# First MLP layer of a transformer block on one core: token sums in two column steps, weight sums in place, a fourth and fifth bank for the first four pairs

## The chip, the cores and the metric

The kernel runs on one core of a Trainium2 chip, as one program. The metric is the device time of a launch in microseconds; the profile is one execution of the same program, recorded by the hardware. Engines are named as in the profile: PE multiplies matrices (PEld loads its weights), DVE, ACT and POOL work elementwise, SP issues the DMAs. Each engine takes its instructions in the order of its queue.

## The reference

One block of a streaming encoder on 1024 tokens of width 1024, in float32. Two attention branches are merged and projected; then comes the MLP, whose first layer the change touches:

```python
x = x + rms_norm(merged @ w_o[l], g_post_mix[l])
h = rms_norm(x, g_pre_mlp[l])
u = jnp.square(jax.nn.relu(h @ w_up[l]))        # w_up: 1024 x 4096
x = x + rms_norm(u @ w_down[l], g_post_mlp[l])
```

## The kernel before

**Precision.** Each operand of a product is kept as a rounded part (`hi`, cast by ACT) and the rest (`lo`, subtracted by DVE), and each product is three matmuls: hi by hi, hi by lo, lo by hi. `split` (L606) does both casts; its two lines are L607 and L608.

**The first layer with seven products.** `h @ w_up` is done in blocks of two by two: the weights of one pair of 128-column groups are A11, A12 (in the raw tile f0), A21, A22 (in f1); the tokens are B11, B12, B21, B22, where the first index is the half of the width and the second the half of the tokens. Instead of eight block products there are seven, of sums of blocks: the token sums T1 to T4 (`T1 = B12 - B11`, `T2 = B22 - T1`, `T3 = B22 - B12`, `T4 = B21 - T2`) are made once, the weight sums for each pair on POOL. A product of blocks is 12 matmuls of 512 columns. The results are put together in a pair by adds on DVE (v, q, u12, u21, u22), then relu and square on ACT. There are 16 pairs (`up_pair`, L768). The products B11 and B21 need only the first half of the tokens, so for the first four pairs (AHEAD) they are done early: each gives p1 (copied out of its bank by ACT, L737) and u11. `accs` there is in the two banks of tag "acc", and the B21 product goes on in the bank that p1 was copied from.

**What stands around the change.** `finish_tile` (L647) does the output projection of one 128-token tile: 48 matmuls, squares on ACT (L108), a scale factor on POOL (L116, L117), scaling and residual on DVE (L668, L669), squares of the result on ACT, a second factor on POOL (L114, L117), the scaling of h on DVE (L674), eight transposes on PE (L679), a copy on ACT (L681) and a store of the transposed blocks to `h_dram` (L682). After the eighth tile, all four token blocks are loaded again from `h_dram` (L753), T1 and T2 made on DVE, T3 and T4 on POOL, for each half q of the rows, and then POOL makes the first pair's weight sums (L772 to L775).

**Order.** The lines are scheduled by the framework before the launch, by its own time model; what comes out is a fixed queue for each engine with waits on semaphores. Tiles come from pools with a number of buffers (`bufs`); a tile whose buffer is still in use waits. The raw weight tiles have two buffers ("raw"), "row" four, "page" 24.

## Time and profile before

| | |
|---|---|
| median of 3 runs | 1512.61 us (1511.29 to 1513.62) |
| profiled execution | 1511.9 us, span 1510.2 us |
| mean granted TensorE clock | 0.983 |
| PE busy | 1442.4 us (96%) |
| DVE, ACT, POOL busy | 950.0, 740.0, 421.2 us |

All times below are of the profiled execution, from the start of its span. A wait names the instruction that came last by the profile. "x8" is a count of instructions in one row; the rows of a timeline that follow each other closely are merged. The clock is given as a share of 2.4 GHz, so 0.50 is 1.2 GHz.

### The profile page before, as it was taken

Reading aid. Unit: us, or ns where it says so; the run is one execution under the profiler, and the core shown is the slowest. Engines: PE = TensorE matmul, PEld = TensorE weight load, DVE = VectorE, ACT = ScalarE, POOL = GpSimd, SP = SyncE. Lnnn points to the kernel's source line nnn. Section 1 sums busy time; section 2 is a strip of 40 time slices with the busy share of each in tenths; the row PEclk is TensorE's granted clock in tenths of the full one; section 3 lists DMA queues with packets and bytes.
Section 4 is the critical chain, followed back from the end, with each engine's and each line's share of the span. In section 5 each row is a group of like instructions: output and inputs, shape, how many; then the busy total and the mean of one; then the engine's idle time right before and its main releaser. Section 6 shows DMA issues by size and latency. Waiting matters only on the chain. (4 is left out here: it accounts for less than half of the span.)

```text
span 1510.2 us, 20192 instructions
## 1 busy us (share of the span) xinstructions
PE 1442.4 (96%) x7314; PEld 1224.7 (81%) x7314; DVE 950.0 (63%) x1384; ACT 740.0 (49%) x1326; POOL 421.2 (28%) x382
## 2 busy tenths in 40 slices
PE   7999999999999999999999749999999999999993
PEld 6888998898889888888888538788888888888882
DVE  5478988898687857445544464444444587556526
ACT  6456766665565545843334433454445345344311
POOL 2022322220000000000011256766654563434205
PEclk9999999999999999999999869999999999999997
DMA  5332223121332253644367534444446775677615
GB/s 199 88 117 65 69 54 87 56 67 57 105 84 64 77 195 112 216 140 167 112 197 222 187 104 155 153 163 158 160 156 212 251 249 169 206 243 245 201 41 195
DMA packets 94411, 218.93 MB, mean 145 GB/s; under 512 B 9340, under 2 KB 25960, under 8 KB 94312
## 3 DMA queue, kind: packets, MB, share of 16 engines
q1 hardware_dynamic: 94312, 217.66, 44.9%
q8 instruction: 57, 0.93, 0.3%
q14 instruction: 42, 0.34, 0.1%
HBM read 151.28 MB, written 60.31 MB: 140 GB/s over the span
## 5 line engine op out<-in xcount | busy, mean ns | idle before, releaser
L198 PE MATMUL acc_gate<-h_hi,lo_gate 128*128 128x512 f32 x256 | 101.0, 394 | 0.0
L196 PE MATMUL acc_gate<-h_hi,hi_gate 128*128 128x512 f32 x256 | 100.9, 394 | 0.0
L197 PE MATMUL acc_gate<-h_lo,hi_gate 128*128 128x512 f32 x256 | 100.8, 394 | 0.0
L331 DVE TENSOR_TENSOR_SCAN rest<-rest 128x896 f32<-128x896 f32 (+3 forms) x64 | 87.6, 1373 | 20.6 <-POOL rest L326 20.3
L608 DVE TENSOR_TENSOR w_lo<-ws,w_hi 128x1024 fp32r<-128x1024 f32 x32 | 44.9, 1405 | 73.6 <-ACT w_hi L607 64.2
L326 POOL TENSOR_SCALAR_AFFINE_SELECT rest<-rest 128x128 f32<-128x128 f32 x64 | 23.5, 368 | 240.7 <-ACT rest L322 236.3
L608 DVE TENSOR_TENSOR lS_lo<-raw_S,lS_hi 128x1024 fp32r<-128x1024 f32 (+1 forms) x32 | 51.7, 1616 | 38.3 <-ACT lS_hi L607 38.3
L116 POOL TENSOR_SCALAR rstd_o<-s 128x1 f32<-128x1 f32 x8 | 2.8, 354 | 249.1 <-DMA xr<-in_x_dram 211.7
L607 ACT CAST lS_hi<-raw_S 128x1024 fp32r<-128x1024 f32 (+1 forms) x32 | 32.0, 1001 | 79.4 <-DMA raw_S<-s_dramS 43.6
L898 PE MATMUL dS<-rT_hi,lS_lo 128*128 128x512 f32 x180 | 70.0, 389 | 0.0
L898 PE MATMUL dS<-rT_lo,lS_hi 128*128 128x512 f32 x180 | 70.0, 389 | 0.0
L898 PE MATMUL dS<-rT_hi,lS_hi 128*128 128x512 f32 x180 | 70.0, 389 | 0.0
L567 PE MATMUL mix<-y,hi_mix 128*128 128x512 f32 x256 | 68.6, 389 | 0.0
L607 ACT CAST w_hi<-ws 128x1024 fp32r<-128x1024 f32 x32 | 33.5, 1046 | 69.8 <-POOL ws L773 60.9
L394 ACT ACTIVATE s<-s,low 128x896 f32<-128x896 f32 (+7 forms) x64 | 49.7, 777 | 29.7 <-DVE low L389 29.5
L375 POOL MEMSET bias<- 64x64 f32 x4 | 0.6, 144 | 214.4 <-DMA bias<-bias_rows 214.4
L389 DVE CUSTOM_DVE_ANT_0 s<-z,bias 128x512 f32<-128x512 f32 (+3 forms) x64 | 37.0, 586 | 32.4 <-PE z L263 26.6
L723 ACT ACTIVATE u<-u 128x512 f32<-128x512 f32 x48 | 30.2, 630 | 54.8 <-DVE u L802 33.7
L567 PEld LDWEIGHTS mix<-y,hi_mix 128*128 128x128 f32 x256 | 48.0, 188 | 10.0
L198 PEld LDWEIGHTS acc_gate<-h_hi,lo_gate 128*128 128x128 f32 x256 | 48.2, 188 | 9.2
L197 PEld LDWEIGHTS acc_gate<-h_lo,hi_gate 128*128 128x128 f32 x256 | 48.2, 188 | 8.8
L608 DVE TENSOR_TENSOR lA_lo<-raw_A,lA_hi 128x1024 fp32r<-128x1024 f32 (+1 forms) x24 | 35.5, 1478 | 31.4 <-ACT lA_hi L607 30.9
(341 smaller groups left out, 4896.9 us busy)
## 6 DMA issues: line engine op xcount, KB each, us to landing
raw_up<-in_w_up_dram SPq DMA_DIRECT2D x32, 512.0 KB, 3.9
s_dramS<-us SPq DMA_DIRECT2D x60, 256.0 KB, 2.0
raw_S<-s_dramS SPq DMA_DIRECT2D x28, 512.0 KB, 4.5
s_dramA<-u SPq DMA_DIRECT2D x49, 256.0 KB, 3.1
raw_A<-s_dramA SPq DMA_DIRECT2D x21, 512.0 KB, 3.7
raw_gate<-in_w_in_dram SPq DMA_DIRECT2D x16, 512.0 KB, 3.7
gate_dram<-gt SPq DMA_DIRECT2D x32, 256.0 KB, 2.5
y<-y_dram SPq DMA_DIRECT2D x16, 512.0 KB, 6.1
```

The costliest lines, as they stand in the source:

```text
L196: nc.tensor.matmul(acc, w_hi[:, ks], h_hi[k][:, cs], start=(k == 0), stop=False)
L197: nc.tensor.matmul(acc, w_hi[:, ks], h_lo[k][:, cs], start=False, stop=False)
L198: nc.tensor.matmul(acc, w_lo[:, ks], h_hi[k][:, cs], start=False, stop=(k == NK - 1))
L326: nc.gpsimd.affine_select(tl[:, dg], tl[:, dg], pattern=[[-1, P]], compare_op=ALU.is_gt, fill=fill, base=0, channel_multiplier=1,)
L331: nc.vector.tensor_tensor_scan(back, back, back, 1.0, op0=ALU.mult, op1=ALU.bypass)
L389: nc.vector.tensor_tensor_reduce(out=s[:, c0:c1], in0=z, in1=bias[:, S - nk + c0:S - nk + c1], scale=1.0, scalar=BIG if prev is None else ...
L394: e = nc.scalar.activation(s[:, :nk], s[:, :nk], AF.Exp, bias=low, scale=-1.0, accum_out=sums[:, m:m + 1],)
L567: nc.tensor.matmul(accs[i][c], st[:, ks], mv[:, cs], start=(first and k % 4 == 0), stop=(last and k % 4 == 3),)
L607: nc.scalar.copy(hi, raw)
L608: nc.vector.tensor_tensor(lo, raw, f32(hi), op=ALU.subtract)
L723: nc.scalar.activation(dst, src, AF.Relu)
L898: nc.tensor.matmul(accs[t], st[:, e, ts], mv[:, e, :], start=(pp == 0 and e == 0 and i == 0), stop=(pp == PP - 1 and i == 2),)
```

## The change

Five things change in the first layer.

- The token blocks are loaded while the last tile (t = 7) is still being worked on, in `load_h`: of the second token half only the columns of tiles 4 to 6 (EARLY, 384 columns). The last tile's transposes are copied by ACT from PSUM into the remaining 128 columns (LATE) of those tiles and aren't stored.
- All token sums are on DVE, first for the EARLY, then for the LATE columns. B22 and T2 come first, then T1, T3, T4. B11 and B21 blocks are loaded whole.
- The weight sums (`sums`) are made in place in the raw tiles f0 and f1, with one extra half tile s1; `split_sums` splits them. S1 is `w1`; f0 becomes S2 and S4 (`w24`), f1 becomes S3 and A22 (`w32`).
- The first pair's sums are made after tile 5's code, ahead of the early products.
- In the first four pairs, B22 and T4 have banks of their own (e and f, tag "acc") instead of going on in the banks of T1 and T3, the order of the products is T2, T1, B22, T3, T4, and the adds are regrouped. The later pairs keep their order.

The diff, without the branch of the later pairs, whose lines are as before but for the names of the weights:

```diff
@@ -657,6 +657,8 @@
                         accs[n], st, mv[:, n * HALF:(n + 1) * HALF],
                         start=(first and k == 0), stop=(last and k == NK - 1),
                     )
+        if t == NT - 1:
+            load_h()
         xt, o = row(f"xr_{t}"), row(f"or_{t}")
         nc.sync.dma_start(out=xt, in_=x[t * P:(t + 1) * P, :])
         s2 = pb.tile([P, 2], F32, tag="ssq", name=f"s2_{t}", bufs=4)
@@ -677,6 +679,10 @@
             for i in range(4):
                 k = 4 * j + i
                 nc.tensor.transpose(tr[:, i * P:(i + 1) * P], o[:, k * P:(k + 1) * P], ident)
+            if t == NT - 1:
+                for q in range(2):
+                    nc.scalar.copy(hraw[j, 1, q][:, :, LATE], tr[:, q * 256:(q + 1) * 256].rearrange("p (k t) -> p k t", k=2))
+                continue
             ht = tmp_tile(f"ht_{t}_{j}")
             nc.scalar.copy(ht, tr)
             nc.sync.dma_start(out=h_dram[j][c][:, :, ts], in_=ht.rearrange("p (k t) -> p k t", k=4))
@@ -693,6 +699,44 @@
         hi, lo = page(f"wa_hi{n}"), page(f"wa_lo{n}")
         split(hi, lo, raw)
         return hi, lo
+    EARLY, LATE = slice(0, HALF - P), slice(HALF - P, HALF)
+    hraw = {}
+    def load_h():
+        for q in range(2):
+            for j, c in ((0, 1), (0, 0), (1, 1), (1, 0)):
+                make = wide if q == 0 else pair_f32 if c else row_pair
+                hraw[j, c, q] = make(f"hraw{j}{c}{q}")
+                cs = EARLY if c else slice(0, HALF)
+                nc.sync.dma_start(out=hraw[j, c, q][:, :, cs], in_=h_block(j, c, q)[:, :, cs])
+    def pair_f32(name):
+        return pair_page(name, F32)
+    def row_pair(name):
+        return row(name, [P, 2, HALF])
+    def sums(n, s1):
+        f0, f1 = (raw_up(2 * n + i, f"up{n}_{i}") for i in range(2))
+        wa = None if n < AHEAD else split_f0(n, f0)
+        a11, a12, a21, a22 = (f[:, i * HALF:(i + 1) * HALF] for f in (f0, f1) for i in range(2))
+        nc.gpsimd.tensor_tensor(s1, a21, a22, op=ALU.add)
+        nc.gpsimd.tensor_tensor(a21, a11, a21, op=ALU.subtract)
+        nc.gpsimd.tensor_tensor(a11, s1, a11, op=ALU.subtract)
+        nc.gpsimd.tensor_tensor(a12, a12, a11, op=ALU.subtract)
+        return n, wa, s1, f0, f1
+    def split_sums(n, wa, s1, f0, f1):
+        w1 = pair_page(f"w1_{n}")
+        split(w1[:, 0, :], w1[:, 1, :], s1)
+        w24 = page(f"w24_hi{n}"), page(f"w24_lo{n}")
+        split(*w24, f0)
+        w32 = page(f"w32_hi{n}"), page(f"w32_lo{n}")
+        split(*w32, f1)
+        return wa, (w1[:, 0, :], w1[:, 1, :]), w24, w32
     first_a = []
     for t in range(NT):
@@ -706,6 +750,8 @@
                     split_h(name, q, raw)
             for n in range(AHEAD):
                 first_a.append(split_f0(n, raw_up(2 * n, f"ahead{n}")))
+        if t == 5:
+            sums0 = sums(0, stream.tile([P, HALF], F32, tag="tmp", name="s1_0", bufs=1))
     def product(acc, a, b, first=True):
@@ -740,76 +786,78 @@
             relu2(u11s[i][:, e, :], accs[e])
             state.append((p1s[i][:, e, :], u11s[i][:, e, :]))
-    def any_h_page(name):
-        made_h.append(name)
-        return big_pair(name) if len(made_h) <= 8 else pair_page(name)
-    made_h = []
-    for name in ("T2", "T1", "T3", "B22", "T4"):
-        h_pages(name, any_h_page)
-    for q in range(2):
-        b12, b11, b22, b21 = (wide(f"hraw_{n}{q}") for n in ("B12", "B11", "B22", "B21"))
-        for tile_, j, c in ((b12, 0, 1), (b11, 0, 0), (b22, 1, 1), (b21, 1, 0)):
-            nc.sync.dma_start(out=tile_, in_=h_block(j, c, q))
-        t2 = row(f"hraw_T2{q}", [P, 2, HALF])
-        nc.vector.tensor_tensor(b11, b12, b11, op=ALU.subtract)
-        nc.vector.tensor_tensor(t2, b22, b11, op=ALU.subtract)
-        split_h("T2", q, t2)
-        nc.gpsimd.tensor_tensor(b12, b22, b12, op=ALU.subtract)
-        split_h("T3", q, b12)
-        split_h("T1", q, b11)
-        split_h("B22", q, b22)
-        nc.gpsimd.tensor_tensor(b21, b21, t2, op=ALU.subtract)
-        split_h("T4", q, b21)
+    weights0 = split_sums(*sums0)
+    for name, make in (("B22", big_pair), ("T2", big_pair), ("T1", pair_page), ("T3", pair_page), ("T4", pair_page)):
+        h_pages(name, make)
+    for cs in (EARLY, LATE):
+        def split_part(name, q, raw):
+            hi, lo = hb[name][q]
+            split(hi[:, :, cs], lo[:, :, cs], raw)
+        hs = [[hraw[j, c, q][:, :, cs] for j, c in ((0, 1), (0, 0), (1, 1), (1, 0))] for q in range(2)]
+        for q, (b12, b11, b22, b21) in enumerate(hs):
+            nc.vector.tensor_tensor(b11, b12, b11, op=ALU.subtract)
+            split_part("B22", q, b22)
+            nc.vector.tensor_tensor(b12, b22, b12, op=ALU.subtract)
+            nc.vector.tensor_tensor(b22, b22, b11, op=ALU.subtract)
+            split_part("T2", q, b22)
+        for q, (b12, b11, b22, b21) in enumerate(hs):
+            split_part("T1", q, b11)
+        for q, (b12, b11, b22, b21) in enumerate(hs):
+            split_part("T3", q, b12)
+        for q, (b12, b11, b22, b21) in enumerate(hs):
+            nc.vector.tensor_tensor(b21, b21, b22, op=ALU.subtract)
+            split_part("T4", q, b21)
     STORED = ("A11", "S1", "S2", "A22", "S3", "S4", "A12")
     def up_pair(n):
-        f0, f1 = (raw_up(2 * n + i, f"up{n}_{i}") for i in range(2))
-        s12, s34 = (row(f"w{s}_{n}", [P, 2, HALF]) for s in ("s12", "s34"))
-        a11, a12, a21, a22 = (f[:, i * HALF:(i + 1) * HALF] for f in (f0, f1) for i in range(2))
-        nc.gpsimd.tensor_tensor(s12[:, 0, :], a21, a22, op=ALU.add)
-        nc.gpsimd.tensor_tensor(s12[:, 1, :], s12[:, 0, :], a11, op=ALU.subtract)
-        nc.gpsimd.tensor_tensor(s34[:, 0, :], a11, a21, op=ALU.subtract)
-        nc.gpsimd.tensor_tensor(s34[:, 1, :], a12, s12[:, 1, :], op=ALU.subtract)
         ahead = n < AHEAD
-        if not ahead:
-            wa = split_f0(n, f0)
-        w12 = page(f"w12_hi{n}"), page(f"w12_lo{n}")
-        split(*w12, s12.rearrange("p a b -> p (a b)"))
-        w34 = page(f"w34_hi{n}"), page(f"w34_lo{n}")
-        split(*w34, s34.rearrange("p a b -> p (a b)"))
-        w22 = pair_page(f"w22_{n}")
-        split(w22[:, 0, :], w22[:, 1, :], a22)
-        b, c, d = (bank(tag, f"p_{tag}{n}") for tag in BANKS[1:])
+        wa, w1, w24, w32 = weights0 if n == 0 else split_sums(*sums(n, row(f"s1_{n}", [P, HALF])))
         u1, u2 = wide(f"u1_{n}"), wide(f"u2_{n}")
         u12, u21, u22 = u1[:, 1, :], u2[:, 0, :], u2[:, 1, :]
+        v, q = tmp_tile(f"v_{n}"), tmp_tile(f"q_{n}")
+        b, c, d = (bank(tag, f"p_{tag}{n}") for tag in BANKS[1:])
         if ahead:
             p1, u11 = state[n]
+            e, f = (bank("acc", f"p{i}_{n}") for i in (3, 4))
+            product(b, blocks(w24, 0), "T2")
+            nc.vector.tensor_tensor(v, b, p1, op=ALU.add)
+            product(c, w1, "T1")
+            nc.vector.tensor_tensor(u12, c, v, op=ALU.add)
+            product(e, blocks(w24, 1), "B22")
+            nc.vector.tensor_tensor(u12, e, u12, op=ALU.add)
+            relu2(u12, u12)
+            product(d, blocks(w32, 0), "T3")
+            nc.vector.tensor_tensor(q, d, v, op=ALU.add)
+            nc.vector.tensor_tensor(u22, c, q, op=ALU.add)
+            relu2(u22, u22)
+            product(f, blocks(w32, 1), "T4")
+            nc.vector.tensor_tensor(u21, f, q, op=ALU.add)
+            relu2(u21, u21)
         else:
             u11 = u1[:, 0, :]
             a = bank("acc", f"c11_{n}")
             product(a, blocks(wa, 0), "B11")
             p1 = tmp1(f"p1_{n}")
             nc.scalar.copy(p1, a)
...
         parts = {"A11": u11, "A12": u21, "A22": u22}
         if n < UP - 1:
```


What the scheduler makes of it on POOL, around the last tile (`rstd_o7` and `rstd_x27` are its two scale factors, `raw_up0_1` the second raw weight tile of pair 0). First POOL's queue before:

```order
L117 TENSOR_TENSOR rstd_x26_8804<-rstd_x26_8804,neg_half_74 128x1
L116 TENSOR_SCALAR rstd_o7_8880<-s2_7_8877 128x1
L117 TENSOR_TENSOR rstd_o7_8880<-rstd_o7_8880,neg_half_74 128x1
L114 TENSOR_SCALAR rstd_x27_8889<-sx_7_8887 128x1
L117 TENSOR_TENSOR rstd_x27_8889<-rstd_x27_8889,neg_half_74 128x1
L758 TENSOR_TENSOR hraw_B120_9045<-hraw_B220_9047,hraw_B120_9045 128x1024
L762 TENSOR_TENSOR hraw_B210_9048<-hraw_B210_9048,hraw_T20_9053 128x1024
L758 TENSOR_TENSOR hraw_B121_9068<-hraw_B221_9070,hraw_B121_9068 128x1024
L772 TENSOR_TENSOR ws12_0_9095<-raw_up0_1_9093 128x512
```

Here the two factors follow each other, then come subtractions on token blocks and only then the sums of pair 0. POOL's queue at the same place after:

```order
L117 TENSOR_TENSOR rstd_x26_8813<-rstd_x26_8813,neg_half_74 128x1
L726 TENSOR_TENSOR s1_0_8739<-raw_up0_1_8742 128x512
L727 TENSOR_TENSOR raw_up0_1_8742<-raw_up0_0_8740,raw_up0_1_8742 128x512
L116 TENSOR_SCALAR rstd_o7_8905<-s2_7_8902 128x1
L728 TENSOR_TENSOR raw_up0_0_8740<-s1_0_8739,raw_up0_0_8740 128x512
L117 TENSOR_TENSOR rstd_o7_8905<-rstd_o7_8905,neg_half_74 128x1
L729 TENSOR_TENSOR raw_up0_0_8740<-raw_up0_0_8740 128x512
L114 TENSOR_SCALAR rstd_x27_8914<-sx_7_8912 128x1
L117 TENSOR_TENSOR rstd_x27_8914<-rstd_x27_8914,neg_half_74 128x1
L726 TENSOR_TENSOR s1_1_9229<-raw_up1_1_9232 128x512
```

Two of pair 0's four sums now stand ahead of the factor's first operation, one between its two operations and one behind; the subtractions on token blocks are gone from POOL.

On SP, the DMA queue, from the loads for the early products to the token blocks (`xr_7` is the last tile's x, `hraw` the token blocks, `x2_dram` where the residual is stored). First SP's queue before:

```order
L661 DMA xr_7_8874<-in_x_dram 128x1024
L689 DMA raw_ahead3_8563<-in_w_up_dram 128x1024
L682 DMA h_dram01_89<-ht_5_0_8728 512x1x128
L682 DMA h_dram11_91<-ht_5_1_8736 512x1x128
L670 DMA x2_dram_87<-xr_6_8789 128x1024
L689 DMA raw_up0_0_9091<-in_w_up_dram 128x1024
L689 DMA raw_up0_1_9093<-in_w_up_dram 128x1024
L682 DMA h_dram01_89<-ht_6_0_8813 512x1x128
L682 DMA h_dram11_91<-ht_6_1_8821 512x1x128
```

Here `xr_7` is loaded early and no token block yet. SP's queue at the same place after:

```order
L713 DMA hraw001_8893<-h_dram00_88 128x1024
L695 DMA raw_ahead3_8563<-in_w_up_dram 128x1024
L713 DMA hraw101_8897<-h_dram10_90 128x1024
L688 DMA h_dram01_89<-ht_5_0_8728 512x1x128
L688 DMA h_dram11_91<-ht_5_1_8736 512x1x128
L672 DMA x2_dram_87<-xr_6_8798 128x1024
L695 DMA raw_up0_0_8740<-in_w_up_dram 128x1024
L695 DMA raw_up0_1_8742<-in_w_up_dram 128x1024
L663 DMA xr_7_8899<-in_x_dram 128x1024
L688 DMA h_dram01_89<-ht_6_0_8822 512x1x128
L688 DMA h_dram11_91<-ht_6_1_8830 512x1x128
L713 DMA hraw010_8883<-h_dram01_89 128x2x384
```

Two whole token blocks now stand ahead of the raw weight loads of pair 0, and the load of `xr_7` has moved behind them.

On DVE, from the last tile's first scaling (L671 after, L669 before) on, with `hT20` and `hB220` the parts of T2 and B22 for q = 0. First DVE's queue before:

```order
L669 SCALAR_TENSOR_TENSOR xr_7_8874<-or_7_8875,rstd_o7_8880,xr_7_8874 128x1024
L674 SCALAR_TENSOR_TENSOR or_7_8875<-xr_7_8874,rstd_x27_8889,grow1_8179 128x1024
L755 TENSOR_TENSOR hraw_B110_9046<-hraw_B120_9045,hraw_B110_9046 128x1024
L756 TENSOR_TENSOR hraw_T20_9053<-hraw_B220_9047,hraw_B110_9046 128x1024
L608 TENSOR_TENSOR hT20_lo_9026<-hraw_T20_9053,hT20_hi_9025 128x1024
L608 TENSOR_TENSOR hT10_lo_9030<-hraw_B110_9046,hT10_hi_9029 128x1024
```

Here the scaling of h comes second, and the token sums only after it. DVE's queue at the same place after:

```order
L671 SCALAR_TENSOR_TENSOR xr_7_8899<-or_7_8900,rstd_o7_8905,xr_7_8899 128x1024
L800 TENSOR_TENSOR hraw000_8885<-hraw010_8883,hraw000_8885 128x2x384
L802 TENSOR_TENSOR hraw010_8883<-hraw110_8887,hraw010_8883 128x2x384
L676 SCALAR_TENSOR_TENSOR or_7_8900<-xr_7_8899,rstd_x27_8914,grow1_8179 128x1024
L608 TENSOR_TENSOR hB220_lo_9060<-hraw110_8887,hB220_hi_9059 128x2x384
L800 TENSOR_TENSOR hraw001_8893<-hraw011_8891,hraw001_8893 128x2x384
L803 TENSOR_TENSOR hraw110_8887<-hraw110_8887,hraw000_8885 128x2x384
L802 TENSOR_TENSOR hraw011_8891<-hraw111_8895,hraw011_8891 128x2x384
L810 TENSOR_TENSOR hraw100_8889<-hraw100_8889,hraw110_8887 128x2x384
L800 TENSOR_TENSOR hraw000_8885<-hraw010_8883,hraw000_8885 128x2x128
L800 TENSOR_TENSOR hraw001_8893<-hraw011_8891,hraw001_8893 128x2x128
```

Two EARLY subtractions stand ahead of the scaling of h (L676, before L674), and the sums of both steps are mixed with the splits.

## Rows read from the trace of the kernel before

**Rows 1.** The page's part 2: PE and its clock in 40 slices, tenths.
```profile
PE   7999999999999999999999749999999999999993
...
PEclk9999999999999999999999869999999999999997
```

**Rows 2.** Waits of PE, 858 to 1210 us: total, times, longest.
```profile
PE p_sc L717 <- ACT w_hi L607: 30.0, 1, 30.0
PE p_av L717 <- DVE u L802: 2.0, 2, 1.1
PE p_tr L717 <- DVE q L800: 0.4, 1, 0.4
PE p_sc L717 <- DVE w_lo L608: 0.3, 1, 0.3
```

**Rows 3.** Windows: busy (instructions) of PE, PEld, DVE, ACT, POOL; PE clock, DMA share, GB/s.
```profile
838.00:840.00 2.00, 2.00 (x10) 1.66 (x9) 0.94 (x1) 1.61 (x3) 0.00 (x0) 1.00 0.99 320
858.00:860.00 2.00, 0.06 (x1) 0.00 (x0) 0.89 (x2) 1.42 (x2) 2.00 (x1) 1.00 0.14 54
860.00:862.00 2.00, 0.00 (x0) 0.00 (x0) 2.00 (x2) 2.00 (x4) 2.00 (x2) 0.54 0.00 0
880.00:890.00 10.00, 1.90 (x4) 1.16 (x4) 9.94 (x5) 2.88 (x3) 9.10 (x4) 0.50 0.00 1
```

**Rows 4.** Chain that ended last, pieces from 835 to 895: start, us, what.
```profile
835.38 10.92 PE c L717 x48
...
866.30 5.90 DMA hraw_B<-h_dram
...
890.31 4.39 PE p_sc L717 x10
```

**Rows 5.** Timeline of DVE: start, us, line, operation, out<-in, idle before.
```profile
837.65 1.28 DVE L669 SCALAR_TENSOR_TENSOR xr<-or,rstd_o,xr 128x1024 f32<-128x1024 f32 x1 [0.34 <-POOL rstd_o L117]
841.11 1.28 DVE L674 SCALAR_TENSOR_TENSOR or<-xr,rstd_x,grow 128x1024 f32<-128x1024 f32 x1 [2.17 <-POOL rstd_x L117]
...
859.66 2.18 DVE L608 TENSOR_TENSOR hT_lo<-hraw_T,hT_hi 128x1024 fp32r<-128x1024 f32 x1 [1.11 <-ACT hT_hi L607]
...
867.33 1.21 DVE L608 TENSOR_TENSOR hT_lo<-hraw_B,hT_hi 128x1024 fp32r<-128x1024 f32 x1
...
891.43 0.68 DVE L608 TENSOR_TENSOR w<-raw_up,w 128x512 fp32r<-128x512 f32 x1
```

**Rows 6.** Timeline of ACT, last token tile.
```profile
838.97 1.06 ACT L108 ACTIVATE or<-xr 128x1024 f32<-128x1024 f32 x1 [0.23 <-DVE xr L669]
...
840.88 0.59 ACT L737 COPY p<-c 128x512 f32<-128x512 f32 x1 [0.76 <-PE c L717]
```

**Rows 7.** Timeline of POOL: a scale factor, then the first sum of five pairs.
```profile
836.68 0.30 POOL L116 TENSOR_SCALAR rstd_o<-s 128x1 f32<-128x1 f32 x1 [4.45 <-ACT or L108]
...
877.03 2.25 POOL L772 TENSOR_TENSOR ws<-raw_up 128x512 f32<-128x512 f32 x1
...
895.81 1.29 POOL L772 TENSOR_TENSOR ws<-raw_up 128x512 f32<-128x512 f32 x1 [6.63 <-DMA raw_up<-in_w_up_dram]
...
908.08 1.29 POOL L772 TENSOR_TENSOR ws<-raw_up 128x512 f32<-128x512 f32 x1 [7.14 <-DMA raw_up<-in_w_up_dram]
...
925.07 1.28 POOL L772 TENSOR_TENSOR ws<-raw_up 128x512 f32<-128x512 f32 x1 [4.96 <-DMA raw_up<-in_w_up_dram]
...
941.53 1.30 POOL L772 TENSOR_TENSOR ws<-raw_up 128x512 f32<-128x512 f32 x1 [4.39 <-DVE u L808]
```

**Rows 8.** SP issuing raw weight loads; single DMAs: KB, us to landing.
```profile
831.52 3.52 SPq L689 DMA_DIRECT2D raw_up<-in_w_up_dram  x2
...
raw_up<-in_w_up_dram SPq DMA_DIRECT2D x1, 512.0 KB, 4.8
...
h_dram<-ht SPq DMA_DIRECT2D x2, 256.0 KB, 5.2
...
hraw_B<-h_dram SPq DMA_DIRECT2D x2, 512.0 KB, 5.0
```

More of the change, by code (lines that the diff above doesn't have):

```diff
@@ L795, in up_pair @@
             nc.scalar.copy(p1, a)
-        product(b, blocks(w12, 1), "T2")
-        v, q = tmp_tile(f"v_{n}"), tmp_tile(f"q_{n}")
-        nc.vector.tensor_tensor(v, b, p1, op=ALU.add)
-        product(d, blocks(w34, 0), "T3")
-        nc.vector.tensor_tensor(q, d, v, op=ALU.add)
-        product(c, blocks(w12, 0), "T1")
-        nc.vector.tensor_tensor(u22, c, q, op=ALU.add)
-        relu2(u22, u22)
-        if not ahead:
+            product(b, blocks(w24, 0), "T2")
+            nc.vector.tensor_tensor(v, b, p1, op=ALU.add)
+            product(d, blocks(w32, 0), "T3")
+            nc.vector.tensor_tensor(q, d, v, op=ALU.add)
+            product(c, w1, "T1")
+            nc.vector.tensor_tensor(u22, c, q, op=ALU.add)
+            relu2(u22, u22)
             product(a, blocks(wa, 1), "B21", first=False)
             relu2(u11, a)
-        product(c, blocks(w34, 1), "B22", first=False)
-        nc.vector.tensor_tensor(u12, c, v, op=ALU.add)
-        relu2(u12, u12)
-        product(d, (w22[:, 0, :], w22[:, 1, :]), "T4", first=False)
-        nc.vector.tensor_tensor(u21, d, v, op=ALU.add)
-        relu2(u21, u21)
+            product(c, blocks(w24, 1), "B22", first=False)
+            nc.vector.tensor_tensor(u12, c, v, op=ALU.add)
+            relu2(u12, u12)
+            product(d, blocks(w32, 1), "T4", first=False)
+            nc.vector.tensor_tensor(u21, d, v, op=ALU.add)
+            relu2(u21, u21)
         parts = {"A11": u11, "A12": u21, "A22": u22}
```

## The prediction, made blind

> **What bounds the kernel now.** I read the page's forty slices first. PE is full nearly everywhere and dips once, in slices 23 and 24, where the granted clock dips with it [rows 1]. Then the waits of PE over the whole first MLP layer: of 32.7 us waited, 30.0 is one wait, for the cast of the first pair's weight sums, and 2.7 are three small ones in the next pairs [rows 2]. Then the windows and the chain through the gap: PE runs the 96 matmuls that need only the first token half, ending at 858.1; the second set of token blocks lands only at 866.30 + 5.90 = 872.2, POOL begins the first pair's weight sums at 877.03, and PE restarts at 890 - 1.9 = 888.1 [rows 3, 4, 7]. Last the clock: 1.00 in the 2 us in which PE's last matmul ended, 0.54 in the next two [rows 3]. After the gap the first 14 matmuls (4 before 890, then 10 in 4.39 us) take about 0.44 us each, against 10.92/48 = 0.2275 at full clock [rows 3, 4]: 14 x 0.21 = 3.0 us more. So this place costs 30.0 + 3.0 + 2.7 = 35.7 us, and outside it the layer is PE alone. That is all the change can win.
>
> **What goes.** The last token tile's transposes no longer travel out to memory and back; ACT copies them into the loaded blocks. Three quarters of the second half's columns (EARLY) and all of the first half are loaded before that tile is done, so the 5.0 and 5.9 us loads [rows 4, 8] leave the path. The eight subtractions of the token sums all go to DVE, so its splits no longer run beside POOL's: 2.18 us beside it, 1.21 alone [rows 5]. The first pair's weight sums move ahead of the gap. PE's work does not change: the number of products is the same, and the extra banks only reorder them.
>
> **What is put in the way: the last token tile.** Before, POOL did nothing around 836 but that tile's two scale factors: the first started at 836.68 and the DVE operation waiting for it at 837.65, 0.97 us later [rows 5, 7]. Now POOL's queue has two of the first pair's block sums ahead of that factor, one inside it and one behind it, and the first of them waits for the second raw weight load. That load is the last of two issued in a stretch that ends at 831.52 + 3.52 = 835.0, and took 4.8 us [rows 8]: 839.5. A 512 KB token block now goes ahead of it in SP's queue, while the DMA engines are 0.99 busy at 320 GB/s [rows 3]: 524/320 = 1.6 us, so 841. (Bounds: 839.5 if it fits into slack, 844 if two such transfers get ahead.) Three sums at 1.25 from start to start (895.81's 1.29 less overlap) and the 0.97: the DVE operation starts at 841 + 3.75 + 0.97 = 845.7, 8 us later than before. The tile's x rows, now loaded only behind that weight load (about 836), land by 842 at its 4.8 us and stay hidden; if they land after 845.7 the stall below grows by as much.
>
> What queues behind it is the cost. On ACT the tile's squares (1.06) stand ahead of the copy of the second early product (0.59), and PE may not overwrite that bank before the copy. Before, squares and copy were at 838.97 and 840.88, and PE never waited [rows 6]. Now the squares start 1.3 after DVE, at 847.0, and the copy ends at 848.6. PE reaches that place after 36 matmuls, 835.4 + 36 x 0.2275 = 843.6, so it waits **5.0 us** (bounds 2 and 9). Before, the clock fell about 2 us into an idle stretch and 14 matmuls then ran slow [rows 3, 4]; after 5 us I take the same **3.0 us** (bound below: 0).
>
> **The token sums themselves.** From the tile's last normalisation on DVE to the split that lets PE go beyond its first four new matmuls, DVE's queue has 10 operations of 768 columns, 12 of 256, one of 512 and one of 1024. By a line through 0.68 and 1.21 [rows 5] that is 10 x 0.95 + 12 x 0.42 + 0.68 + 1.21 = 16.6 us, less some 0.08 overlap each, about 15. Before, that normalisation started 2.14 us after the tile's squares (841.11 against 838.97 [rows 5, 6]), which would now be 849.1; and, new, two EARLY subtractions stand ahead of it and wait for the token loads. These follow the previous tile's stores (issued about 836.5, landing 5.2 later, 842) and land in pairs 5.0 later [rows 8]: 847 to 848. So it starts at about 849, ends at 850.3, and the split ends at 865.5 to 867. PE after its stall has 12 + 48 matmuls and 0.8 us of transposes: 848.6 + 60 x 0.2275 + 0.8 + 3.0 = 866.0. They meet: I take **0** for this wait, with 0 to 4 as bounds. If the front stall is absent PE comes at 858 and waits here instead, since DVE's 15 us do not shrink.
>
> **The first pairs.** The two raw buffers are now held until the split of the sums made in them. Before, the second buffer was already held until the last split, and it paced the pairs: POOL's first sum starts at 895.81, 908.08, 925.07 and 941.53, 12.3, 17.0 and 16.5 us apart, against 60 x 0.2275 = 13.7 of PE work per pair [rows 7]. PE's waits there were 2.7. That pacing stays as it was. New is that the second pair's sums come while DVE still splits T3 and T4, where a POOL operation takes 2.25 instead of 1.29 [rows 7]: four times 0.96 = 3.8 us later, some of it covered. With the slow-clock lead gone I take **3.6 us** of waits (bounds 1 and 10).
>
> One rule bears on this last point: the Trainium skill, "SBUF — State Buffer", section on who interferes with whom, says that a VectorE operation with two SBUF inputs and a GpSimd one that reads SBUF exclude each other, so one waits for the whole of the other. The trace agrees (2.18 and 2.25 where they meet). By the rule taken strictly, the six splits left by then (about 4.1 us) and the four sums (5.0) run one after the other, so the second pair's weights would come 4.1 us late, not 3.8, and the sum would change by 0.3.
>
> **Sum.** The new losses are 5.0 + 3.0 + 0 + 3.6 = 11.6 us against 35.7: 24.1 less. The profiled execution took 1511.9 (span 1510.2), so 1487.8; the median of the runs is 0.7 above the profiled one, so 1488 to 1488.5. The pairs from the fifth on have 84 matmuls, 19.1 us, and stay PE's.
>
> **Rivals.**
> 1. *The front is covered.* If the weight load lands at 839.5 and the sums run unhindered, DVE starts at 844.2, PE waits 3.5 us, and a shorter idle may leave the clock up, with 1 to 2 us of waiting at T2 instead: losses of 4 to 6, 1481 to 1483. For it: PE's waits of 1 us after the gap left the clock alone [rows 1, 2]. Against: the queue order is fixed, and DMA is full just there.
> 2. *The front is later, or the pairs are paced.* The load at 844 makes the stall 8; or pairs 1 to 3 run at the 16.7 of before instead of 13.7, 3 us each over three pairs: 9 instead of 3.6. Losses of 17 to 22: 1494 to 1499. For it: the measured 17.0 and 16.5. Against: with those PE waited only 2.7, because it does the next pairs' other products between.
> 3. *Slower: summing in place paces all later pairs.* One buffer's cycle is load, four sums, casts, splits, next load, with up to four POOL operations for the stored sums in between. Before, the last two of those four stood behind the cycle; put inside it they add 1.3 + 2.25 to 16.5, 20.0 against PE's 19.1, which over twelve pairs is 11 us (1499 in all). It makes the kernel slower only from 19.1 + 24/12 = 21.1 us per pair on, that is if most POOL operations also run at 2.25. Against: in the new order most later pairs have the four sums first, and a pair's weights are split almost a whole pair ahead.
> 4. *It doesn't do what it says*: T2 still needs the last tile, and if DVE's 15 us were not hidden behind the products, up to 16 of the 30 us would return: 1504. Only the queue's order, not the trace, says they are hidden.
>
> **How the numbers follow.** Forecast 0.62 (1485 to 1492 by its own bounds), rival 1 0.17, rival 2 0.13, rival 4 0.04, rival 3 0.04 (three quarters of it slower). The range 1480 to 1496 leaves out about 0.2. About 0.2% (3 us) is what can be told from no change: faster 0.95, same 0.02, slower 0.03.
>
> **What would show it.** In the new profile: PE's 30 us wait for a weight cast gone; one wait of about 5 us near 843 inside the early products, put down to ACT's copy, with the clock at half after it; POOL's first sum starting near 841, directly on the landing of a raw weight load; DVE's splits of the token sums near their uncontended length; T2 starting near 866 with little wait; 1 to 2 us waits in the second and third pairs; none from the fifth. The forecast is wrong if PE's losses between the last output-projection matmul and the fifth pair are under 7 or over 17 us, or if the later pairs take over 19.3 us each.

## The result, and the profile after

The changed kernel takes 1495.10 us (median of four runs, 1494.08 to 1498.55) against 1511.95 for the kernel before (1510.27 to 1513.62) beside it: a ratio of 0.9893, interval 0.9872 to 0.9913. It is 16.9 us faster; the forecast was 24. The time lies in the forecast's range of 1480 to 1496, at its upper end. The profiled execution took 1494.08 (span 1492.4).

The first page still shows where the place was: in place of the dip to 7 and 4 tenths [rows 1] there are two slices at 8 tenths with a full one between them, and the clock row no longer dips. The first of the two (821 to 858 us) holds the early products, the second (895 to 933 us) the third and fourth pair.

```profile
PE   7999999999999999999999898999999999999993
PEclk9999999999999999999999999999999999999997
```

The waits of PE from the last output projection through the first MLP layer, in the changed kernel (what it waited for: us in total, times, longest), against the 30.0 us of [rows 2]:

```profile
PE c L763 <- ACT p L783: 5.5, 1, 5.5
PE p_sc L763 <- ACT w_hi L607: 3.7, 2, 2.2
PE p_tr L763 <- DVE q L849: 1.2, 1, 1.2
PE p_av L763 <- ACT w L607: 1.1, 2, 0.7
PE p_sc L763 <- DVE w_lo L608: 1.0, 1, 1.0
PE p_av L763 <- DVE u L851: 0.7, 1, 0.7
PE trh L681 <- DVE or L676: 0.6, 1, 0.6
PE p_av L763 <- DVE w L608: 0.5, 1, 0.5
```

The first row belongs to the front (the last token tile among the early products). The seventh lies ahead of the early products, at the transposes of the tile before, where the kernel before waited 0.8 us. The other six, 8.2 us, lie in the pairs, where the forecast had 3.6: 6.3 of them come before the fifth pair, 1.9 behind its start.

The front, in the timeline of the changed kernel (start, us, engine, line, operation, in brackets the idle time before it and its releaser), one fence for each engine. POOL:

```profile
840.61 1.28 POOL L726 TENSOR_TENSOR s<-raw_up 128x512 f32<-128x512 f32 x1 [7.89 <-DMA xr<-in_x_dram]
843.36 0.30 POOL L116 TENSOR_SCALAR rstd_o<-s 128x1 f32<-128x1 f32 x1
...
845.49 1.26 POOL L729 TENSOR_TENSOR raw_up<-raw_up 128x512 f32<-128x512 f32 x1
```

DVE, ACT and PE behind it:

```profile
845.56 2.27 DVE L671 SCALAR_TENSOR_TENSOR xr<-or,rstd_o,xr 128x1024 f32<-128x1024 f32 x1 [7.75 <-POOL rstd_o L117]
847.87 1.06 ACT L108 ACTIVATE or<-xr 128x1024 f32<-128x1024 f32 x1 [8.62 <-DVE xr L671]
848.92 0.57 ACT L783 COPY p<-c 128x512 f32<-128x512 f32 x1
866.46 0.39 PE L763 MATMUL p_sc<-hT_hi,w_hi 128*128 128x512 f32 x1
```

POOL does two sums of the raw weights, then the scale factor with a third sum inside it. (The first row names the x rows, but the second raw weight tile, which this sum reads, was issued at 835.20 and landed 5.3 us later, at 840.5, just before the sum starts.) DVE waits for the factor, ACT's squares wait for DVE, and the copy of the product stands behind the squares. PE is back at 849.54 and reaches T2 at 866.46 without a wait. The clock in that stretch, by windows of the changed kernel (us, PE busy, PEld, DVE, ACT, POOL, PEclk, DMA share, GB/s):

```profile
845.00:850.00 5.00, 0.46 (x1) 0.46 (x2) 3.97 (x3) 2.13 (x4) 2.57 (x5) 0.76 1.02 353
850.00:855.00 5.00, 5.00 (x16) 3.84 (x16) 4.54 (x6) 1.48 (x4) 0.65 (x1) 0.55 0.79 279
919.40:922.50 3.10, 3.10 (x7) 2.48 (x8) 2.17 (x1) 0.00 (x0) 3.02 (x2) 0.50 0.85 242
```

After the 5.5 us wait 12 matmuls take 5.29 us in the chain, 2.6 more than at 0.2275 each. The third row is one pair's start, told below.

Losses are counted in one way from here on, from PE's timeline: the time that a stretch took, less its matmuls at 0.2267 us each (84 of them take 19.04 us in the later pairs, where PE waits for nothing). So a loss holds both PE's waits and what half clock costs. The front is the stretch from the start of the first early product to that of T2; its 96 matmuls and eight transposes (0.8 us) make 22.6 us. The pairs are counted from T2 on, the first four pairs (240 matmuls) by themselves. So counted, the front loses 8.1 us, the first four pairs 10.2 and the later ones 2.6, 20.9 together. Before, it was 30.3, 4.3 (most of it half clock behind the gap) and 3.5, or 38.1. The difference is 17.2; the measured gain is 16.9.

The pairs, POOL's first sum of each from the second on, in the changed kernel:

```profile
874.04 3.73 POOL L726 TENSOR_TENSOR s<-raw_up 128x512 f32<-128x512 f32 x1 [23.39 <-DVE hT_lo L608]
...
890.63 1.30 POOL L726 TENSOR_TENSOR s<-raw_up 128x512 f32<-128x512 f32 x1
891.89 1.31 POOL L867 TENSOR_TENSOR us<-us,u 128x512 f32<-128x512 f32 x1
...
894.85 1.30 POOL L869 TENSOR_TENSOR us<-u,us 128x512 f32<-128x512 f32 x1
...
909.83 1.29 POOL L726 TENSOR_TENSOR s<-raw_up 128x512 f32<-128x512 f32 x1 [3.98 <-DMA raw_up<-in_w_up_dram]
...
926.49 1.30 POOL L726 TENSOR_TENSOR s<-raw_up 128x512 f32<-128x512 f32 x1 [3.78 <-DMA raw_up<-in_w_up_dram]
```

The four sums (L726) stand 16.6, 19.2 and 16.7 us apart; in [rows 7] it was 12.3, 17.0 and 16.5. The fourth and the fifth wait for a transfer of raw weights. In the third pair two other sums, of the layer's results (L867, L869), stand between the pair's own, 2.6 us in all, as much as its 19.2 has over the others' 16.6. What lies between two of them, on ACT, DVE and SP's queue:

```profile
882.24 2.00 ACT L607 CAST w_hi<-raw_up 128x1024 fp32r<-128x1024 f32 x2 [3.81 <-POOL raw_up L729]
883.32 2.36 DVE L608 TENSOR_TENSOR w_lo<-raw_up,w_hi 128x1024 fp32r<-128x1024 f32 x2 [2.45 <-ACT w_hi L607]
884.57 1.46 SPq L695 DMA_DIRECT2D raw_up<-in_w_up_dram  x2
```

The sums end at 882.21; then two casts and two splits, and the third pair's loads go out from 884.57 on, as the splits end. Its sums start at 890.63. PE meets the end of that cycle three times (the same kernel's PE):

```profile
899.88 0.50 PE L763 MATMUL p_sc<-hT_hi,w_hi 128*128 128x512 f32 x1 [2.19 <-ACT w_hi L607]
917.18 0.50 PE L763 MATMUL p_sc<-hT_hi,w_hi 128*128 128x512 f32 x1 [1.53 <-ACT w_hi L607]
919.40 0.79 PE L763 MATMUL p_sc<-hT_hi,w_lo 128*128 128x512 f32 x1 [1.02 <-DVE w_lo L608]
```

The forecast's sum was 24.1 and about 17 came, so 7 us are missing. Two candidates: the front (8.1 against 8.0 forecast, a visible stall, behind which everything else stands), and the cycle of the two raw tiles, which summing in place holds until cast and split have read them.

### The profile page after: what moved, and what is told of

Same layout as the page of the kernel before. It is cut to its first block, busy times and chain, and to the rows that moved or that the text cites. A ratio compares the mean times of both kernels' runs of the same rounds, so it can differ in the third digit from the quotient of the medians.

```text
span 1492.4 us, 20173 instructions
## 1 busy us (share of the span) xinstructions
PE 1443.9 (97%) x7314; PEld 1224.5 (82%) x7314; DVE 955.7 (64%) x1410; ACT 739.4 (50%) x1338; POOL 414.4 (28%) x378
## 5 line engine op out<-in xcount | busy, mean ns | idle before, releaser
L608 DVE TENSOR_TENSOR w_lo<-raw_up,w_hi 128x1024 fp32r<-128x1024 f32 x32 | 44.4, 1397 | 49.8 <-ACT w_hi L607 43.3
L763 PE MATMUL c<-hB_hi,wa_hi 128*128 128x512 f32 x128 | 51.0, 398 | 5.5 <-ACT p L783 5.5
L196 PEld LDWEIGHTS acc_gate<-h_hi,hi_gate 128*128 128x128 f32 x256 | 48.2, 188 | 8.6
```

What stands on the lines that cost most here:

```text
L196: nc.tensor.matmul(acc, w_hi[:, ks], h_hi[k][:, cs], start=(k == 0), stop=False)
L608: nc.vector.tensor_tensor(lo, raw, f32(hi), op=ALU.subtract)
L763: nc.tensor.matmul(acc, st[:, ks], mv, start=(first and k == 0 and i == 0), stop=(k == 3 and i == 2), skip_group_check=True,)
```

## Experiments

Every ratio is against the kernel before, run beside it. Losses are in us, of the profiled execution, as counted above; the last column is the time in us from the start of the first early product (835.72 in the changed kernel) to that of T2 (866.46), so that it doesn't depend on when the stage began. The front's loss is this time less 22.6.

| run | us | ratio (95%) | front loss | first four pairs | later pairs | early products to T2 |
|---|---|---|---|---|---|---|
| changed kernel | 1495.10 | 0.9893 (0.9872 to 0.9913) | 8.1 | 10.2 | 2.6 | 30.7 |
| factors first | 1495.12 | 0.9891 (0.9875 to 0.9906) | 7.3 | 11.2 | 3.2 | 29.9 |
| two sets | 1484.35 | 0.9817 (0.9800 to 0.9833) | 8.3 | 3.9 | 0.1 | 30.9 |
| own tiles | 1487.70 | 0.9842 (0.9824 to 0.9860) | 8.5 | 6.1 | 0.4 | 31.1 |
| three banks | 1498.99 | 0.9915 (0.9900 to 0.9929) | 7.8 | 14.0 | 4.3 | 30.4 |
| last weights split in halves | 1494.55 | 0.9873 (0.9853 to 0.9893) | 7.9 | 6.7 | 5.8 | 30.5 |
| two tiles on chip | 1485.73 | 0.9818 (0.9797 to 0.9840) | 9.7 | 3.9 | 0.1 | 32.3 |
| blocks in pages | 1487.97 | 0.9832 (0.9815 to 0.9850) | 10.7 | 4.1 | 0.0 | 33.3 |
| tokens behind the tile | 1486.51 | 0.9821 (0.9804 to 0.9837) | 9.2 | 4.5 | 0.0 | 31.8 |
| sums before tokens | 1483.98 | 0.9817 (0.9801 to 0.9834) | 6.6 | 5.3 | 0.0 | 29.2 |

**The front alone: the scale factors ahead of the sums.** POOL does the last tile's two factors, then the first pair's four sums (`last_pow` is the operation that makes a factor, so in the end the last one).

```diff
-        if t == 5:
-            sums0 = sums(0, stream.tile([P, HALF], F32, tag="tmp", name="s1_0", bufs=1))
+    with tc.issue_after(getattr(last_pow[0], "ins", last_pow[0])):
+        sums0 = sums(0, stream.tile([P, HALF], F32, tag="tmp", name="s1_0", bufs=1))
...
```

> The first pair's four sums queue on POOL behind both factors of the last tile. Theory (the stall at the front only moves: T2 cannot start much before 865, because the token blocks land at 847 to 849 and DVE then has some 15 us of sums and splits, and the pairs behind it go at the pace of their raw buffers, 16.6 us): the 5.5 us wait for ACT's copy becomes about 3 us at the first copy, since the squares still wait for x (landing about 841), a new wait of 2 to 4 us stands ahead of T2, and the time falls by 0 to 2 us, to 1493 to 1495. Rival (the stall is a loss of its own): 5.5 us of wait and 2.4 us of half clock come back, 1487.

Measured: 1495.12, the time of the changed kernel. The wait that was to go got shorter and split up, as the waits of PE in this run show:

```profile
PE c L765 <- ACT p L785: 5.1, 2, 3.5
PE p_sc L765 <- ACT w_hi L609: 3.1, 2, 1.5
PE p_sc L765 <- DVE w_lo L610: 1.9, 2, 1.0
```

T2 comes 0.9 us sooner (29.86 against 30.73), and the pairs lose 1.6 more. So the sums inside the factor do cause part of the stall, but taking them out is worth nothing by itself, as the theory had it: PE comes sooner to work that isn't ready sooner.

**The pairs, a second set of raw tiles.** The second raw tile of every pair but the first gets its own memory (a free row tile), so that loads need no longer wait for the split of the pair before.

```diff
-        f0, f1 = (raw_up(2 * n + i, f"up{n}_{i}") for i in range(2))
+        f0 = raw_up(2 * n, f"up{n}_0")
+        if n == 0:
+            f1 = raw_up(1, "up0_1")
+        else:
+            f1 = row(f"raw_up{n}_1")
+            nc.sync.dma_start(out=f1, in_=w_up[2 * n + 1])
```

> From the second pair on, one of the two raw weight tiles is a row tile, so two pairs' weights are held at a time instead of one. Theory (pairs 1 to 3 are paced by load, four sums in place, casts, splits and the next load in one set of buffers, 16.6 to 19.2 us against 13.7 us of PE work): PE's waits from the second pair on fall from about 11 us with the half clock to 1 to 4, and the time to 1485 to 1488; the front stall of 5.5 us stays. Rival (POOL's eight sums a pair, or the contention with DVE, set the pace): the waits stay above 8 us, 1492 to 1495.

Measured: 1484.35, 10.7 us less than the changed kernel and just below what the theory gave, with the front as it was. The waits of PE:

```profile
PE c L768 <- ACT p L788: 5.3, 1, 5.3
PE c L768 <- DVE u L836: 1.3, 1, 1.3
PE p_tr L768 <- DVE hT_lo L608: 1.3, 1, 1.3
...
PE p_sc L768 <- DVE w_lo L608: 0.5, 1, 0.5
```

No wait of over 0.5 us for weights is left. The pairs' loss falls from 12.8 to 4.0, in the first four from 10.2 to 3.9. The rival (POOL's sums, or its contention with DVE, set the pace) is out: POOL does the same sums, and the first of them takes even longer here. POOL's sums of the second, third and fourth pair begin thus (the same run):

```profile
859.65 11.78 POOL L731 TENSOR_TENSOR s<-raw_up 128x512 f32<-128x512 f32 x1 [9.31 <-DMA raw_up<-in_w_up_dram]
880.75 1.29 POOL L731 TENSOR_TENSOR s<-raw_up 128x512 f32<-128x512 f32 x1 [3.97 <-DVE hT_lo L608]
887.14 1.30 POOL L731 TENSOR_TENSOR s<-raw_up 128x512 f32<-128x512 f32 x1 [1.17 <-DVE w_lo L608]
```

The third and fourth start 9.9 and 22.7 us earlier than at 890.63 and 909.83. The pacing by the raw tiles is gone.

**The pairs, sums in their own tiles again.** Pairs from the second on sum as before, into four own halves, and T2's weights are split from those; the rest of the change stays.

```diff
+        if n == 0:
...
+        s12, s34 = (row(f"w{s}_{n}", [P, 2, HALF]) for s in ("s12", "s34"))
+        nc.gpsimd.tensor_tensor(s12[:, 0, :], a21, a22, op=ALU.add)
+        nc.gpsimd.tensor_tensor(s12[:, 1, :], s12[:, 0, :], a11, op=ALU.subtract)
+        nc.gpsimd.tensor_tensor(s34[:, 0, :], a11, a21, op=ALU.subtract)
+        nc.gpsimd.tensor_tensor(s34[:, 1, :], a12, s12[:, 1, :], op=ALU.subtract)
+        return n, wa, s12, s34, a22
```

> From the second pair on the weight sums go into two tiles of their own, as in the kernel before, and the raw tiles are free as soon as they are read; all else stays changed. Theory (making the sums in place holds both raw tiles for a cast and a split longer, and T2 waits for all four sums): first sums of pairs 1 to 3 come 12 to 17 us apart again, PE's waits in these pairs fall by 4 to 7 us, 1488 to 1491. Rival (the first pairs wait only because PE now asks for them without a gap ahead; in place or not is the same): waits as in the changed kernel, 1493 to 1496.

Measured: 1487.70, 7.4 us less than the changed kernel, just below what the theory gave. The first sums of the pairs (POOL in this run) stand 16.4, 16.0 and 15.9 us apart:

```profile
877.45 3.59 POOL L733 TENSOR_TENSOR ws<-raw_up 128x512 f32<-128x512 f32 x1 [23.89 <-DMA raw_up<-in_w_up_dram]
893.82 1.29 POOL L733 TENSOR_TENSOR ws<-raw_up 128x512 f32<-128x512 f32 x1
909.80 1.30 POOL L733 TENSOR_TENSOR ws<-raw_up 128x512 f32<-128x512 f32 x1 [0.32 <-DMA raw_up<-in_w_up_dram]
925.72 1.29 POOL L733 TENSOR_TENSOR ws<-raw_up 128x512 f32<-128x512 f32 x1 [1.10 <-DMA raw_up<-in_w_up_dram]
```

From the first to the fourth that is 48.3 us; in the changed kernel it is 52.5, before 45.7. This run undoes one part of the change, summing in place, and lands near the forecast's 1488. The front is hardly touched (8.5), the pairs lose 6.5 instead of 12.8.

**The banks.** The old order of the products, with three banks instead of five, in the first four pairs.

```diff
-            e, f = (bank("acc", f"p{i}_{n}") for i in (3, 4))
...
-            product(e, blocks(w24, 1), "B22")
-            nc.vector.tensor_tensor(u12, e, u12, op=ALU.add)
+            product(c, w1, "T1")
...
+            product(c, blocks(w24, 1), "B22", first=False)
+            nc.vector.tensor_tensor(u12, c, v, op=ALU.add)
```

> In the first four pairs B22 and T4 go on in the banks of T1 and T3 again, in the order T2, T3, T1, B22, T4; all else stays changed. Theory (raw buffers set the pace, and PE's work ahead of each pair's T2 is the same 192 or so matmuls either way): 1493 to 1497, the waits moved but not less than 8 us. Rival (the five banks and their order took away the other products with which PE bridged the weights before): 1488 to 1491, waits under 5 us from the second pair on.

Measured: 1498.99, 3.9 us more than the changed kernel and above what either the theory or the rival gave. The two ratio intervals overlap, so the size is uncertain; PE's timeline has some 5.5 us more lost in the pairs. Where, in PE's waits:

```profile
PE p_av L763 <- DVE w L608: 4.8, 2, 4.3
```

In the changed kernel PE's queue has the first pairs' B22 products ahead of T1's. Here B22 goes on in T1's bank, so T1's weights are wanted first, and they aren't split yet: a wait of 4.3 us, and half clock behind it (a window of this run, columns as above):

```profile
884.00:888.00 4.00, 4.00 (x10) 3.14 (x11) 2.30 (x3) 1.41 (x3) 0.00 (x0) 0.50 0.23 28
```

In the changed kernel the same release costs 0.5. So the two more banks are worth some 4 us here, through the order that they allow.

**The fourth sum.** The last weights are split in two halves, so that the half that doesn't need the fourth sum goes first.

```diff
-        split(*w24, f0)
+        for cols in (slice(0, HALF), slice(HALF, S)):
+            split(w24[0][:, cols], w24[1][:, cols], f0[:, cols])
```

> The tile that holds S2 and S4 is cast and split in two halves instead of one, so that T2 of a pair waits for three of its four sums instead of all; the sums stay in place. Theory (the hold of the raw tiles is the larger part of what summing in place costs, the wait for the fourth sum, 1.3 us and half a cast a pair, the smaller): T2 of the third and fourth pairs comes 1 to 3 us earlier, 1492 to 1494. Rival (T2's wait for the fourth sum is what costs): nearly all that tiles of their own give back, 1488 to 1490.

Measured: 1494.55, not to be told from 1495.10, and near the theory. But the pairs' loss, 12.5 instead of 12.8, is a balance of two parts: the first four lose 6.7 instead of 10.2, and the later ones 5.8 instead of 2.6, there in waits for results on DVE and ACT. So T2's wait for the fourth sum may be worth up to 3.5 us in the first four pairs (one profile); why the later pairs lose about as much is not tested. The cycle of the raw tiles hardly moves: from the second pair's first sum to the fifth's it is 51.8 us instead of 52.5. What holds the tiles is not the one last sum but all of sums, cast and split together.

**Is there more in an earlier T2?** Four kernels build on factors first and two sets, each on the one before it, and try to bring the token blocks to DVE sooner. In the first, tile 6 stays on the chip too, so EARLY is the first 256 columns and waits for neither tile's stores.

```diff
+        if t == NT - 2:
+            held.append(o)
+        elif t == NT - 1:
+            keep(t, o)
...
-    EARLY, LATE = slice(0, HALF - P), slice(HALF - P, HALF)
+    EARLY, LATE = slice(0, HALF - 2 * P), slice(HALF - 2 * P, HALF)
```

> On top of e2_two_sets and e1_factors_first: the transposes of tile 6 too stay on the chip, so EARLY and LATE are 256 columns each, and the EARLY blocks can be loaded behind tile 5's stores, some 6 us sooner. Theory (what holds T2 at 866 is the chain of token loads, 15 us of DVE work and the weight casts, and the front stall only fills that time): with the chain begun earlier T2 starts at 859 to 863 and 3 to 7 us come back, 1477 to 1481. What may take it: x of the last tile now lands behind the token blocks, a stall of 1 to 3 us at the copies of the early products; and the first pair's sums on POOL fall into DVE's token work. Rival (T2 is held by something else, the weight casts on ACT): 1483 to 1486.

Measured: 1485.73, no better than two sets alone and where the rival put it. T2 comes after 32.3 us, 1.6 later than in the changed kernel. It waits 0.8 us for a weight cast, the rival's cause, but more is lost where a new wait has taken the place of the old one. First PE's, then DVE's rows of this run:

```profile
PE c L785 <- DVE or L673: 6.1, 1, 6.1
```

```profile
841.52 0.69 DVE L822 TENSOR_TENSOR hraw<-hraw,hraw 128x512 f32<-128x512 f32 x1 [6.17 <-DMA hraw<-h_dram]
...
842.86 1.28 DVE L673 TENSOR_TENSOR or<-o,grow 128x512 f32<-128x512 f32 x2
```

Two token subtractions that wait for their blocks until 841.52 stand in DVE's queue ahead of the operation that reads PE's bank and frees it.

The second moves two of the eight token blocks out of row tiles into page tiles, so that x of the last tile, which needs a row tile, can be loaded earlier.

```diff
-                make = wide if q == 0 else pair_f32 if c else row_pair
+                make = wide if q == 0 else pair_f32
```

> As e6_two_tiles_on_chip, and two token blocks that held row tiles are put into page tiles, so that x of the last tile is loaded some 10 us earlier. Theory: the stall at the early copies goes (below 1 us), T2 starts at 858 to 861, 1475 to 1479, if the first pair's sums, whose second raw tile is now loaded only behind eight token blocks (landing near 845), are not kept waiting by DVE. Rival (they are: in e2_two_sets one POOL sum beside a run of DVE splits took 11.78 us): T2 waits for the casts of the first pair's weights, 3 to 8 us, 1480 to 1485.

Measured: 1487.97, outside both ranges. The x rows are issued at 826.1 instead of 837.8, but the same wait for DVE stays (6.3 us), T2 after 33.3 us. The third puts the token subtractions and splits, on DVE and ACT, behind the last tile's operations.

```diff
+    with tc.issue_after(getattr(last_dve[0], "ins", last_dve[0])), tc.issue_after(getattr(last_act[0], "ins", last_act[0])):
+        for cs in (EARLY, LATE):
...
```

> As e7_blocks_in_pages, with DVE's and ACT's token operations queued behind the last tile's own (its normalisation on DVE, its squares on ACT). Theory (in e6 and e7 two token subtractions that waited for blocks landing at 841.5 stood ahead of the operations that free the last tile's PSUM banks, and cost the 6.1 and 6.3 us that the earlier chain had won): the wait for DVE's L673 operation goes, a stall of 1 to 3 us at the first copies stays, since one ACT cast still waits for a block there, T2 starts at 859 to 864, and the time is 1476 to 1481. Rival (T2 is held by the DVE and POOL work itself, whatever its order): T2 at 865 to 868, 1483 to 1487.

Measured: 1486.51, T2 after 31.8 us, as the rival had it. The wait for DVE's operation is gone, but the front still loses 9.2: PE now waits 2.1 and 3.6 us for ACT's copies of the early products. The second of these copies stands in ACT's queue behind a cast that waits for DVE's token work, and there POOL's sums and DVE's token operations meet, and most of them take longer; POOL and then DVE in this run:

```profile
847.72 1.30 POOL L750 TENSOR_TENSOR s<-raw_up 128x512 f32<-128x512 f32 x1 [8.33 <-DMA raw_up<-in_w_up_dram]
...
855.79 1.73 POOL L753 TENSOR_TENSOR raw_up<-raw_up 128x512 f32<-128x512 f32 x1
```

```profile
847.81 3.46 DVE L825 TENSOR_TENSOR hraw<-hraw,hraw 128x512 f32<-128x512 f32 x2 [0.84 <-ACT hraw L707]
...
859.80 0.68 DVE L828 TENSOR_TENSOR hraw<-hraw,hraw 128x512 f32<-128x512 f32 x1
```

The first row of DVE has two operations in 3.46 us; the second, after POOL's sums, one in 0.68. The fourth kernel also loads the first pair's raw weights ahead of the token blocks, so that the sums are done sooner, and holds ACT's token casts only behind the copies of the first two early products.

```diff
-            load_h()
+            with tc.issue_after(getattr(last_sp[0], "ins", last_sp[0])):
+                load_h()
...
```

> As e8_tokens_behind_tile, but the first pair's raw weights are loaded ahead of the token blocks, so that its four sums on POOL run before most of DVE's token work instead of beside it, and ACT's token casts are queued behind the first two early copies. Theory (in e8 POOL's six sums from 847.7 to 857.5 and DVE's token work took turns, each DVE operation 1.7 instead of 0.68 us, some 5 us in all, and that held T2 at 866): the front stall falls under 1 us, T2 starts at 860 to 864, 1478 to 1483. Rival (DVE's 15 us and the landing of the blocks alone hold T2, or the blocks now land later by the two weight tiles, 3 us): T2 at 865 to 867, 1484 to 1487.

Measured: 1483.98, the lowest of all, but with the ratio of two sets (0.9817). T2 comes after 29.2 us. The front stall, which the theory put under 1 us, is 4.3 in PE's waits:

```profile
PE c L795 <- ACT u L801: 4.3, 1, 4.3
```

DVE waits 3.9 us for a token block, until 849.18; ACT's casts wait for DVE, and the operation that frees PE's bank stands behind the casts.

Against the changed kernel three of the four brought T2 later, the last one 1.6 us sooner; against factors first, which is in all four, that is 0.7. All four lose 4 to 5 us in the pairs, as two sets does; they differ in the front. DVE's token work (15 us in the forecast) begins when the blocks have landed and the last tile is done, and each edit moved one of these or put something else in DVE's way. What a much earlier T2 would be worth was not measured and stays open.

Two sets is the version to keep: it beats both kernels with one small edit, and the further edits of the last four bring no gain on it that can be told from none.

## Why the prediction was right in its way and wrong in its size

- *The 30 us wait goes; 35.7 us at the place.* Right. The wait is gone, and the place counted 38.1 by PE's timeline. The forecast left 11.6 us of losses, and 20.9 were left: 9.3 more, of which 2.4 are made up by the larger place.
- *The front, 5.0 + 3.0.* Right, by its own steps. POOL's first sum 840.61 (forecast 841), DVE's operation 845.56 (845.7), ACT's squares 847.87 (847.0), the wait 5.5, the slow lead 2.6. The 0.9 us by which the squares were late are DVE's 2.27 us beside POOL's fourth sum, which starts 0.07 us before it; alone it takes 1.28 [rows 5].
- *T2, wait 0, at 866.0.* Right: 866.46, no wait. (The sum of DVE's work is 16.4 us, not the 16.6 written there; "about 15" holds.) With the stall shortened, in the run with the factors first, the time came back as waits for weights behind T2's start.
- *The pairs, 3.6.* Here it failed, and the step is the sentence "That pacing stays as it was." It did not: from the second pair's first sum to the fifth's it was 45.7 us [rows 7] and is 52.5, 6.7 more, which is about the size of what is missing. Before, one raw tile came free with the sums and only the other waited for a split; in place both wait for four sums, a cast and a split. Three pairs of PE's 13.7 us are 41.1, so the pace leaves 11.4 us over, and the first four pairs lost 10.2. With own tiles 7.2 are left over and 6.1 lost. The pace is not the whole of it: with the last weights split in halves it leaves 10.7 over and only 6.7 are lost, and before it left 4.7 over and PE hardly waited, behind its gap of 30 us. Own tiles give back 7.4 us and a second set 10.7, with the front hardly changed in both; the front's own edit gives back nothing. So it is shown by edits on both sides that the missing 7 us lie in the pairs and in the hold of the raw tiles. Of the second set's 10.7 us some 2.5 come from the later pairs.
- *What the pairs were charged for.* The 3.6 came from POOL's sums running beside DVE's splits. That happens, and costs more where it does (3.73 us for the first sum of the second pair), but PE hardly waits there: 0.7 us at 878.5, and nothing at the second pair's T2.
- *Rival 2* came nearest: "pairs 1 to 3 run at the 16.7 of before instead of 13.7". It was put aside because PE had waited only 2.7 us at that pace. That speaks of the old cycle, 45.7 us over three pairs, and not of the new one. Losses up to the fifth pair were about 18 us, over the bound of 17 that the forecast set itself as the sign of being wrong. The time is 3 us above the forecast's own bounds of 1485 to 1492; that it still lies in the range of 1480 to 1496 is owed to the room kept for the rivals.
- *Rival 3* worked out the new cycle, 20.0 us, and applied it only to the later pairs, where PE's work takes 19.1 and nearly covers it. The third pair's cycle measured 19.2, with two of POOL's other sums inside it, as that rival described. The number that the forecast lacked stood in its own rival, beside pairs whose PE work is 13.7. For the later pairs it said no, rightly: they take 19.0 us each but for two of 20.1 and 20.6, whose waits (0.7 us at 1005.4, 1.2 at 1023.7) are for results on DVE, not for weights.
- *The banks.* The forecast had no term for them and called them a reordering. The run with three banks puts some 4 us on them: without them the shortfall would have been about 11 us, not 7.

## What to carry to other kernels

When a buffer is to be worked on in place, write down its whole cycle in us (load, every reader up to the last, reissue) and hold it against the consumer's time in each stage, the shortest first: what is covered in a stage of 19 us is bare in one of 14. If a free tile exists, a second set undoes it with a few lines. A stall that looks like the next bound is only worth its price if what comes behind it is ready sooner too: move it alone once, and look where the time reappears.

## What the runs showed of the hardware

**POOL can be kept out for a whole run of DVE operations.** A 128x512 sum that takes 1.29 us alone took 11.78 in the run with two sets (spans on POOL are rough in a profile). It started at 859.65 and ended at 871.43; DVE in that stretch, in the same run, works nearly without a gap:

```profile
861.49 1.62 DVE L808 TENSOR_TENSOR hraw<-hraw,hraw 128x768 f32<-128x768 f32 x3
...
870.62 0.69 DVE L832 TENSOR_TENSOR v<-p_sc,p 128x512 f32<-128x512 f32 x1 [0.35 <-PE p_sc L768]
```

DVE's first pause in that stretch is the 0.35 us before 870.62; counted back from its end, the sum's own 1.29 us begin at 870.14, about there. Until then POOL alone paid: DVE's operations keep their usual length. In the run with tokens behind the tile the two alternated, and both paid. The Trainium skill, "SBUF — State Buffer", section "Who interferes with whom", says of the port pair that the two engines share: "it's an exclusive lock", and "Issue order, not op shape, decides who blocks." The alternation agrees (1.73 for each of the two); an operation that stays shut out over a whole run of others doesn't follow from the rule as told there.

**The same length of wait left the clock up once and halved it once.** In the changed kernel a wait of 2.19 us at 897.7 was followed by full clock:

```profile
900.00:902.00 2.00, 1.94 (x8) 1.28 (x9) 1.75 (x2) 1.31 (x2) 2.00 (x1) 1.00 0.58 221
```

With own tiles, a wait of 2.2 us ended at 884.6 and was followed by half clock less than 2 us later (a window of that run):

```profile
886.00:888.50 2.50, 2.50 (x8) 1.91 (x7) 2.50 (x4) 1.70 (x3) 0.00 (x0) 0.50 0.56 195
```

And in the changed kernel two shorter ones, 1.53 and 1.02 us with four matmuls between, left the clock at 0.50 from 919.4 on. For a sum, a wait of about 2 us so carries a price from nothing to some 2 us beside its own length; which of the two it will be no run here settles.
